# The intra-chunk scores of a recurrence, computed 64 keys at a time, with the two directions' masked scores added before the output matmuls

## The chip, the cores and the metric

The kernel runs on one core of one Trainium2 chip. The metric is the device time of one execution in microseconds (us), as the median over runs. A trace of one profiled execution of the kernel before the change is at hand.

## What is computed

The reference is one transformer block on 256 tokens of width 2048: a modulated norm, one wide projection, a recurrent branch (a gated linear recurrence that runs over the tokens forwards and backwards), a windowed attention branch, a gated merge and a convolutional feed-forward part. The change lies in the recurrent branch alone. It has eight heads of width 128. The sequence is cut into chunks of 64 tokens, and for each chunk, direction and head the reference computes (b is the running sum of log f inside the chunk)

```python
intra = jnp.einsum('bhncd,bhnsd->bhncs', q * jnp.exp(b - b_ref), k * jnp.exp(b_ref - b))
intra = jnp.where(tri, intra, 0.0)
o_intra = jnp.einsum('bhncs,bhnse->bhnce', intra, v)
...
o_n = jnp.einsum('bhcd,bhde->bhce', q_n, s)
s = d_n[..., None] * s + jnp.einsum('bhsd,bhse->bhde', k_n, v_n)
```

The backward direction is the same on flipped tokens, and the two outputs are added: `rms_norm(o_f + o_b, norm_g)`. So the masked scores of both directions are multiplied by the same values v and end in one sum.

## The kernel before the change

Weights stream from HBM in tiles of eight 128x128 blocks. SyncE (SP) issues the load of `raw` (L111), ScalarE (ACT) writes its rounded upper part `whi` (L112), VectorE (DVE) the rest `wlo` (L113), and TensorE (PE) multiplies with both (`mmul`, L68, in `duo`, `tform_all` and `natural`; results go to the PSUM tiles named `bankm`). This weight stream runs from start to end of the program. The rest is slipped in between: after every four steps of k a `tick()` takes one entry from a list of tasks. The Tile framework then orders the instructions of each engine by priority, so the order on an engine is fixed before the run.

For each head h the recurrent branch has these pieces:

- `hgrn_a(h, d, ps)`, once for each direction d, makes the decayed keys and queries from the projection: `KA` and `KB` are the keys of the two halves of each chunk, with zeros where the other half stands, `E1` the queries, `K_` the keys with the decay to the end of the chunk. `hgrn_q(h)` makes `QC`, the queries that meet the other chunk of a pair, and `K2`. All of it is DVE and ACT work on the tile `hb`.
- `hgrn_b(h)` (L555 to L577 before) computes the scores for two chunks at a time: key blocks of 128 tokens (a = 0, 1) for two directions, four squares of 128 keys by 128 queries in one PSUM bank `ips` (`banks<-hb` in the profile). For each square one matmul has all 128 keys of `KA` as weights and 128 queries moving, and a second has all 128 of `KB` and the 64 queries of one half of each chunk. Then four matmuls at L569 with 64 keys and 64 queries write the quarter of each square between its two chunks. One `copy_predicated` at L572 on DVE takes the four squares under a mask into `MI`, and six transposes at L576 (weights `hb`, `cst` is the identity in the names) turn the keys for the state update, which ACT copies out at L577.
- `hgrn_c(h)` (L579 to L588) updates the states: six matmuls at L584 and L585, then DVE at L586 and L588.
- `hgrn_d(h)` (L590 to L602) computes the output in one PSUM tile: four matmuls of `vn` with `MI` (`banks<-hb,vn`), one for each direction and key block, and four with the states `SS` (`banks<-hb`).
- `hgrn_e(h)` normalises the output one head later (L604 to L610).

All these matmuls are in fp32: each stands in the trace as two records (two passes), each with a weight load. A transpose has one record. The weight stream's matmuls (`bankm`) have one record each.

Two other users appear in the rows. `ada_mm` near the start multiplies 32 columns of weights (`csr`) with 256 or 512 moving columns; its sixteen steps of k are written to partitions 0, 32, 64 and 96 in turn. `ada()` (L378 to L398) is background work on DVE, with transposes at L391.

Of the kernel before, what the change touches and what calls it, by code (L numbers as in the profile page):

```python
# [9 lines left out]
U32 = mybir.dt.uint32  # L10
AF = mybir.ActivationFunctionType
ALU = mybir.AluOpType
AX = mybir.AxisListType

P = 128
# [6 lines left out]
CH = 64  # L22
# [28 lines left out]
def block_kernel(ctx, tc, xct, prm, cst, ada2, wst, out):  # L51
    nc = tc.nc
    V, S, PE = nc.vector, nc.scalar, nc.tensor
# [9 lines left out]
    def bank(pool=None):  # L63
        pool = pool or mm
        return pool.tile([P, 512], F32, name="bank" + ("m" if pool is mm else "s"))

    def mmul(o, l, r, start, stop):
        return PE.matmul(o, l, r, start=start, stop=stop, skip_group_check=True)  # L68
# [23 lines left out]
    def con(n):  # L92
        o, w = COFF[n]
        return cst_t[:, o:o + w]
# [85 lines left out]
    start = big.tile([P, 1024], F32, name="csr", tag="acc")  # L180
# [14 lines left out]
    def ada_mm(aps, u):  # L195
        n, per = len(chunks[u]), 4 // len(chunks[u])
        w = 256 * n
        for kt in range(KT):
            g, slot = 32 * (kt % 4), slots[groups[u][kt // 8 if n == 2 else 0] % 3][kt // per % 4]
            last_mm = mmul(aps[g:g + 32, 0:w], csr[:, kt, :], slot[:, kt % per * w:(kt % per + 1) * w], kt < 4, kt >= KT - 4)  # L200
        return last_mm
# [17 lines left out]
    def warm(n, after):  # L219
        with tc.issue_after(after.ins):  # L220
            for _ in range(n):
                last = mmul(ssq[:, 0:P], ident, ident, True, True)
        return last
# [35 lines left out]
    with tc.high_priority(offset=RUSH):  # L259
        for cnd in range(2):  # L260
            ts = slice(T * cnd, T * cnd + T)
# [4 lines left out]
    first = ada_mm(aps, 0)  # L266
    with tc.high_priority(offset=RUSH):
        first = warm(3, first)
# [9 lines left out]
    def unit(u):  # L278
        if len(chunks[u]) == 1:
            st.load(7)  # L280
            wv, w = [st.next(4)], [st.next() for _ in range(3)]
        else:
            st.load()
            wv = [st.next(4) for _ in range(2)]
            st.load(6)
            w = [st.next() for _ in range(6)]
        st.pos = 8
        return wv, w
# [19 lines left out]
    for u in range(len(chunks)):  # L308
        wv, w = unit(u)
# [42 lines left out]
    vn = big.tile([P, 4, 1024], F32, name="vn", tag="v")  # L352
# [121 lines left out]
    def carve():  # L474
        pos = [0]

        def take(n):
            r = hb[:, pos[0]:pos[0] + n]
            pos[0] += n
            return r  # L480
        return take

    take = carve()
    A_ = take(1024).rearrange("p (d t) -> p d t", d=2)
    K_ = take(1024).rearrange("p (d t) -> p d t", d=2)
    B_ = take(1024).rearrange("p (d t) -> p d t", d=2)
    E1 = take(512).rearrange("p (d t) -> p d t", d=2)
    KA = take(512).rearrange("p (d t) -> p d t", d=2)
    KB = take(512).rearrange("p (d t) -> p d t", d=2)
    QI = take(512).rearrange("p (d t) -> p d t", d=2)  # L490
    QC = take(256).rearrange("p (d a t) -> p d a t", d=2, a=2)
    K2 = take(256).rearrange("p (d t) -> p d t", d=2)
    KN = take(768).rearrange("p (d a e) -> p d a e", d=2, a=3)
    MI = take(512).rearrange("p (d a e) -> p d a e", d=2, a=2)
    SS = take(512).rearrange("p (n d e) -> p n d e", d=2, n=2)
    OS = take(512).rearrange("p (d t) -> p d t", d=2)
    for zt in (MI, KA, KB):
        V.memset(zt, 0.0)
# [54 lines left out]
            V.tensor_tensor(decb[:, d:d + 1], dec4[:, d, d, 0:1], dec4[:, d, d, 1:2], op=ALU.mult)  # L553

    def hgrn_b(h):  # L555
        ips = bank(ms)
        for d in range(2):
            for a in range(2):
                ts = slice(a * P, a * P + P)
                io = ips[:, (2 * d + a) * P:(2 * d + a + 1) * P]  # L560
                ih = io.rearrange("p (c h t) -> p c h t", c=2, h=2)[:, :, 1 - d, :]
                eh = E1[:, d, ts].rearrange("p (c h t) -> p c h t", c=2, h=2)[:, :, 1 - d, :]
                mmul(io, KA[:, d, ts], E1[:, d, ts], True, False)
                mmul(ih, KB[:, d, ts], eh, False, True)

        for d in range(2):
            c1, c2 = CH * d, CH * (1 - d)
            for a in range(2):
                PE.matmul(ips[c1:c1 + CH, (2 * d + a) * P + c2:(2 * d + a) * P + c2 + CH],  # L569
                          K_[:, d, a * P + c1:a * P + c1 + CH], QC[:, d, a], start=True, stop=True, skip_group_check=True)  # L570
        hm = con("hmask").bitcast(U32).rearrange("p (d e) -> p d e", d=2)[:, :, None, :].broadcast_to([P, 2, 2, P])
        V.copy_predicated(MI, hm, ips.rearrange("p (d a e) -> p d a e", d=2, a=2))  # L572
        for d in range(2):
            tp = bank(ms)
            for a, k in enumerate((K_[:, d, T:T + P], K_[:, d, T + P:], K2[:, d])):
                PE.transpose(tp[:, a * P:(a + 1) * P], k, ident)  # L576
            S.copy(KN[:, d], tp[:, 0:3 * P].rearrange("p (a e) -> p a e", a=3))  # L577

    def hgrn_c(h):  # L579
        hs = slice(h * P, h * P + P)  # L580
        sp = bank(ms).rearrange("p (n d e) -> p n d e", n=2, d=2)
        for d in range(2):
            for a in range(2):
                PE.matmul(sp[:, 0, d], KN[:, d, a], vn[:, 2 + a, hs], start=(a == 0), stop=(a == 1))  # L584
            PE.matmul(sp[:, 1, d], KN[:, d, 2], vn[:, d, hs], start=True, stop=True)  # L585
        V.tensor_copy(SS[:, 0], sp[:, 0])  # L586
        for d in range(2):
            V.scalar_tensor_tensor(SS[:, 1, d], SS[:, 0, d], decb[:, d:d + 1], sp[:, 1, d], op0=ALU.mult, op1=ALU.add)  # L588

    def hgrn_d(h):  # L590
        hs = slice(h * P, h * P + P)
        ob = bank(ms)
        obs[h] = ob
        first = True
        for d in range(2):
            for a in range(2):
                mmul(ob[:, a * P:a * P + P], vn[:, a, hs], MI[:, d, a, :], first, False)
                first = False
        for d in range(2):
            for a in range(2):  # L600
                mmul(ob[:, a * P:a * P + P], SS[:, a ^ d, d], QI[:, d, a * P:a * P + P], False, d == 1)
        S.activation(OS[:, 0], ob[:, 0:T], AF.Square)  # L602
# [58 lines left out]
    for h in range(H):  # L661
# [14 lines left out]
        for d in range(2):  # L676
            if 2 * h + d < 3:
                o = early_f[2 * h + d]
            else:
                o = bank()  # L680
                tform_all(o)
            hgrn_a(h, d, o)
            ada(1 if h > 5 or not h else 2)
        hgrn_q(h)
        parts = [lambda h=h: hgrn_e(h - 1), lambda h=h: hgrn_b(h), lambda h=h: hgrn_c(h), lambda h=h: hgrn_d(h)]
        if h == 0:

# [269 lines left out]
def _constants(np):  # L957
    c = np.zeros((P, CW), np.float32)

    def put(n, a):  # L960
        o, w = COFF[n]
        c[:, o:o + w] = a
    put("ident", np.eye(P, dtype=np.float32))
    put("ones", 1.0)
    pos = np.arange(T)
    inv = (np.float32(10000.0) ** (-np.arange(32, dtype=np.float32) / np.float32(32))).astype(np.float32)
    ar = ((pos // 64).astype(np.float32)[:, None] * inv).astype(np.float32)
    ac = ((pos % 64).astype(np.float32)[:, None] * inv).astype(np.float32)
    cc = np.concatenate([np.cos(ar), np.cos(ar), np.cos(ac), np.cos(ac)], 1)
    ss = np.concatenate([-np.sin(ar), np.sin(ar), -np.sin(ac), np.sin(ac)], 1)  # L970
    put("ropec", cc.reshape(2, P, P).transpose(1, 0, 2).reshape(P, 256))
    put("ropes", ss.reshape(2, P, P).transpose(1, 0, 2).reshape(P, 256))
    i, j = np.arange(P)[:, None], np.arange(P)[None, :]
    put("amask", np.concatenate([np.where(j <= i, 0.0, NEG), np.where(j >= i, 0.0, NEG)], 1))
    put("hmask", np.concatenate([i <= j, i >= j], 1).astype(np.float32))
    m = np.ones((1, T), np.float32)
    m[0, ::CH] = 0.0
    put("m64", m)
    return c
# [104 lines left out]
```

## Time and profile before

| | us |
|---|---|
| median of 3 runs | 1693.81 (1692.94 to 1693.84) |
| the profiled execution, its own time | 1692.48 |
| its span in the trace | 1690.7 |
| PE busy | 1677.4 (99% of the span) |
| PE weight loads (PEld) busy | 1425.9 (84%) |
| DVE busy | 1202.0 (71%) |
| ACT busy | 836.8 (49%) |

The span runs from the first to the last instruction; about 1.8 us of the execution lie outside it. PE and PEld are the two parts of TensorE, matmuls and weight loads. A record's duration is from its start to the end of its last result, so records of consecutive matmuls overlap: what a matmul costs a busy PE is the distance between starts, not its duration. The eight heads of the recurrence lie between about 134 and 479 us.

### The profile page before, as it was taken

Reading aid. Unit: us, or ns where it says so; the run is one execution under the profiler, and the core shown is the slowest. Engines: PE = TensorE matmul, PEld = TensorE weight load, DVE = VectorE, ACT = ScalarE, POOL = GpSimd, SP = SyncE. Lnnn points to the kernel's source line nnn. Section 1 sums busy time; section 2 is a strip of 40 time slices with the busy share of each in tenths; the row PEclk is TensorE's granted clock in tenths of the full one; section 3 lists DMA queues with packets and bytes.
Section 4 is the critical chain, followed back from the end, with each engine's and each line's share of the span. In section 5 each row is a group of like instructions: output and inputs, shape, how many; then the busy total and the mean of one; then the engine's idle time right before and its main releaser. Section 6 shows DMA issues by size and latency. Waiting matters only on the chain.

```text
span 1690.7 us, 24845 instructions
## 1 busy us (share of the span) xinstructions
PE 1677.4 (99%) x9486; PEld 1425.9 (84%) x9486; DVE 1202.0 (71%) x1896; ACT 836.8 (49%) x1279; POOL 68.8 (4%) x132
## 2 busy tenths in 40 slices
PE   8999999999999999999999999999999999999999
PEld 4668888888888888888888988888888888888887
DVE  3448975665879886878879887778666556666565
ACT  4337543443646664554554665555555435554332
POOL 0000100000000000000100000000000000000000
PEclk9999999999999999999999999999999999999999
DMA  9987733534466667877866577687555555555564
GB/s 379 408 343 257 270 125 129 193 102 152 158 195 204 212 223 245 293 257 267 280 216 232 180 240 261 211 277 250 192 187 188 187 188 188 194 190 187 187 200 149
DMA packets 104152, 371.84 MB, mean 220 GB/s; under 512 B 11488, under 2 KB 13920, under 8 KB 104032
## 3 DMA queue, kind: packets, MB, share of 16 engines
q1 hardware_dynamic: 85600, 303.14, 51.6%
q0 software_dynamic: 18432, 67.12, 12.7%
q8 instruction: 74, 1.21, 0.3%
q14 instruction: 46, 0.38, 0.1%
HBM read 368.11 MB, written 2.10 MB: 219 GB/s over the span
## 4 chain that ended last, share of the span: by engine, by line
PE 97%; DVE 1%; DMA 1%; issue 0%; ACT 0%; SPq 0%; DVEq 0%
PE bankm L68 89%; PE banks L68 6%; DMA ringv<-in_wst_dram 1%; PE banks L584 0%; PE banks L391 0%; PE banks L755 0%; DVE wlo L113 0%; PE banks L576 0%; DMA xraw<-in_xct_dram 0%; PE banks L585 0%; PE banks L209 0%; PE banks L569 0%; PE banks L608 0%; DVE acc L383 0%; PE banks L725 0%
## 5 line engine op out<-in xcount | busy, mean ns | idle before, releaser
L68 PE MATMUL bankm<-hl,whi 128*128 128x512 f32 (+1 forms) x3392 | 1050.6, 392 | 0.0
L113 DVE TENSOR_TENSOR wlo<-raw,whi 128x1024 fp32r<-128x1024 f32 (+1 forms) x498 | 606.5, 1219 | 324.4 <-ACT whi L112 323.0
L112 ACT CAST whi<-raw 128x1024 fp32r<-128x1024 f32 (+1 forms) x498 | 520.4, 1045 | 597.9 <-PE bankm L68 502.3
L68 PEld LDWEIGHTS bankm<-hl,wlo 128*128 128x128 f32 x3104 | 581.4, 188 | 131.9 <-DVE wlo L113 0.2
L68 PE MATMUL bankm<-hl,wlo 128*128 128x256 f32 (+2 forms) x3104 | 660.3, 287 | 0.0
L68 PEld LDWEIGHTS bankm<-hl,whi 128*128 128x128 f32 x3392 | 533.9, 189 | 19.9 <-DVE fs L873 0.3
L68 PE MATMUL bankm<-whi,hl 128*128 128x512 f32 x512 | 164.6, 395 | 1.0 <-ACT hl L230 0.9
L383 DVE SCALAR_TENSOR_TENSOR acc<-araw,csil,acc 128x1024 f32<-128x1024 f32 x120 | 153.3, 1278 | 1.8 <-DMA araw<-in_ada_dram 1.3
L68 PEld LDWEIGHTS bankm<-whi,hl 128*128 128x128 f32 x512 | 95.8, 188 | 22.4 <-ACT hl L230 2.6
L378 POOL DMA_DIRECT2D araw<-in_ada_dram x128 | 68.6, 536 | 1103.7 <-DVE acc L383 590.8
L68 PE MATMUL bankm<-wlo,hl 128*128 128x512 f32 x256 | 99.5, 391 | 0.0
L68 PE MATMUL bankm<-yb,whi 128*128 128x512 f32 x256 | 80.8, 397 | 0.0
L68 PE MATMUL bankm<-g,whi 128*128 128x512 f32 x256 | 80.4, 395 | 0.0
L68 PEld LDWEIGHTS bankm<-g,wlo 128*128 128x128 f32 x256 | 48.1, 188 | 11.4
L68 PEld LDWEIGHTS bankm<-yb,wlo 128*128 128x128 f32 x256 | 48.1, 188 | 11.3
L68 PEld LDWEIGHTS bankm<-wlo,hl 128*128 128x128 f32 x256 | 48.0, 188 | 9.8 <-DVE wlo L113 0.2
L904 DVE SCALAR_TENSOR_TENSOR xm<-bankm,modv,xm 128x256 f32<-128x256 f32 x96 | 42.1, 479 | 18.4 <-PE bankm L68 18.3
L886 ACT ACTIVATE fs<-fs,prm 128x256 f32<-128x256 f32 x44 | 26.5, 601 | 55.9 <-DVE fs L449 55.9
L68 PE MATMUL bankm<-yb,wlo 128*128 128x256 f32 x256 | 50.6, 279 | 0.0
L68 PE MATMUL bankm<-g,wlo 128*128 128x256 f32 x256 | 50.3, 278 | 0.0
L887 DVE SCALAR_TENSOR_TENSOR fs<-fs,prm,fs 128x255 f32<-128x255 f32 x44 | 21.3, 484 | 26.7 <-ACT fs L886 26.7
L211 DVE TENSOR_REDUCE tn<-banks 128x8 f32<-128x32 f32 (+1 forms) x9 | 1.7, 188 | 53.4 <-ACT whi L112 50.5
(218 smaller groups left out, 1227.7 us busy)
## 6 DMA issues: line engine op xcount, KB each, us to landing
raw<-in_wst_dram SPq DMA_DIRECT2D x489, 512.0 KB, 3.4
araw<-in_ada_dram POOLq DMA_DIRECT2D x128, 512.0 KB, 4.7
ringv<-in_wst_dram SPq DMA_DIRECT2D x24, 512.0 KB, 9.9
ringq<-in_wst_dram SPq DMA_DIRECT2D x20, 512.0 KB, 9.9
araw<-in_wst_dram SPq DMA_DIRECT2D x10, 512.0 KB, 9.9
xraw<-in_xct_dram SPq DMA_DIRECT2D x8, 512.0 KB, 6.8
raw<-in_wst_dram SPq DMA_DIRECT2D x7, 384.0 KB, 9.9
ringkT<-in_wst_dram SPq DMA_DIRECT2D x5, 512.0 KB, 9.9
```

The costliest lines, as they stand in the source:

```text
L68: return PE.matmul(o, l, r, start=start, stop=stop, skip_group_check=True)
L112: S.copy(hi, raw)
L113: self.last = V.tensor_tensor(lo, raw, hi.bitcast(F32), op=ALU.subtract)
L211: V.tensor_reduce(m8, aps[:, 0:w].rearrange("p (q g c) -> p q c g", q=2 * n, g=4)[:, :, 0:2, :], axis=AX.X, op=ALU.add)
L378: nc.gpsimd.dma_start(raw, ada2[idx])
L383: V.scalar_tensor_tensor(acc, raw, csil[:, kt, 0:1], acc, op0=ALU.mult, op1=ALU.add)
L886: S.activation(t, s, AF.Identity, bias=cb[:, f:f + 1], scale=cw[:, f, 1:2])
L887: V.scalar_tensor_tensor(t[:, 1:T], s[:, 0:T - 1], cw[:, f, 0:1], t[:, 1:T], op0=ALU.mult, op1=ALU.add)
L904: V.scalar_tensor_tensor(xm[:, j, :], o[:, T * i:T * i + T], gate2[:, j:j + 1], xm[:, j, :], op0=ALU.mult, op1=ALU.add)
```

## The change

`hgrn_b` lays the scores out in two PSUM areas x and y in place of four squares. x holds, for each key block a, one square of 128 keys by 128 queries: its two diagonal quarters have the forward scores inside the chunks, and the other two quarters the scores between the chunks, one quarter of each direction. y holds, for each a, 128 keys by 64 queries: the backward scores inside the chunks. Every matmul has 64 keys as weights and writes 64 partitions, 0 to 63 or 64 to 127, in turn: sixteen with `KA` (64 queries) and `KB` (32 queries), then four between the chunks. DVE masks x with one `copy_predicated` into `MI[:, 0]`, y with two of 64 partitions each into `MI[:, 1]`, and adds both into the new tile `MS`. `hgrn_d` multiplies `vn` with `MS`: two matmuls in place of four. The mask `hmask` in the constants has new values. Nothing else is edited.

```diff
+    MS = take(256).rearrange("p (a e) -> p a e", a=2)
...
     def hgrn_b(h):
         ips = bank(ms)
+        x, y = [ips[:, i * 2 * P:i * 2 * P + w].rearrange("p (a e) -> p a e", a=2) for i, w in ((0, 2 * P), (1, P))]
         for d in range(2):
             for a in range(2):
-                ts = slice(a * P, a * P + P)
-                io = ips[:, (2 * d + a) * P:(2 * d + a + 1) * P]
-                ih = io.rearrange("p (c h t) -> p c h t", c=2, h=2)[:, :, 1 - d, :]
-                eh = E1[:, d, ts].rearrange("p (c h t) -> p c h t", c=2, h=2)[:, :, 1 - d, :]
-                mmul(io, KA[:, d, ts], E1[:, d, ts], True, False)
-                mmul(ih, KB[:, d, ts], eh, False, True)
-
-        for d in range(2):
-            c1, c2 = CH * d, CH * (1 - d)
-            for a in range(2):
-                PE.matmul(ips[c1:c1 + CH, (2 * d + a) * P + c2:(2 * d + a) * P + c2 + CH],
-                          K_[:, d, a * P + c1:a * P + c1 + CH], QC[:, d, a], start=True, stop=True, skip_group_check=True)
-        hm = con("hmask").bitcast(U32).rearrange("p (d e) -> p d e", d=2)[:, :, None, :].broadcast_to([P, 2, 2, P])
-        V.copy_predicated(MI, hm, ips.rearrange("p (d a e) -> p d a e", d=2, a=2))
+                for kx, eh in ((KA, 0), (KB, CH // 2)):
+                    for c in range(2):
+                        ks, q0, w = slice(a * P + CH * c, a * P + CH * c + CH), (1 - d) * eh, CH - eh
+                        o = (y[CH * c:CH * c + CH, a, :] if d else x[CH * c:CH * c + CH, a, CH * c:CH * c + CH])[:, q0:q0 + w]
+                        mmul(o, kx[:, d, ks], E1[:, d, ks][:, q0:q0 + w], not eh, bool(eh))
+        for a in range(2):
+            for d in range(2):
+                c1, c2 = CH * d, CH * (1 - d)
+                mmul(x[c1:c1 + CH, a, c2:c2 + CH], K_[:, d, a * P + c1:a * P + c1 + CH], QC[:, d, a], True, True)
+        hm = con("hmask").bitcast(U32)
+        V.copy_predicated(MI[:, 0], hm[:, None, 0:P].broadcast_to([P, 2, P]), x)
+        for c in (0, CH):
+            V.copy_predicated(MI[c:c + CH, 1, :, c:c + CH], hm[c:c + CH, None, P:P + CH].broadcast_to([CH, 2, CH]), y[c:c + CH])
+        V.tensor_tensor(MS, MI[:, 0], MI[:, 1], op=ALU.add)
...
-        first = True
-        for d in range(2):
-            for a in range(2):
-                mmul(ob[:, a * P:a * P + P], vn[:, a, hs], MI[:, d, a, :], first, False)
-                first = False
+        for a in range(2):
+            mmul(ob[:, a * P:a * P + P], vn[:, a, hs], MS[:, a, :], a == 0, False)
```

The order that the framework writes for PE at the first head's scores and output. A row gives line, operation, tiles, and the output's shape (partitions x columns). Before:

```order
L68 MATMUL banks<-hb 128x128
L68 MATMUL banks<-hb 128x2x32
...
L569 MATMUL banks<-hb 64x64 x4
L576 MATMUL banks<-cst,hb 128x128 x6
...
L68 MATMUL banks<-hb,vn 128x128 x4
L68 MATMUL banks<-hb 128x128 x4
```

Now:

```order
L68 MATMUL banks<-hb 64x64 x2
L68 MATMUL banks<-hb 64x32 x2
...
L68 MATMUL banks<-hb 64x64 x4
L581 MATMUL banks<-cst,hb 128x128 x6
...
L68 MATMUL banks<-hb,vn 128x128 x2
L68 MATMUL banks<-hb 128x128 x4
```

The pairs of the first two rows are repeated four times in both. The block stands at the same place in the weight stream in heads 0 to 6. In heads 2 and 5 one transpose of the background work (L391) stands inside the block, behind its first matmul, before and now.

The last head on PE, before:

```order
L576 MATMUL banks<-cst,hb 128x128 x2
L68 MATMUL banks<-hb 128x128
L68 MATMUL banks<-hb 128x2x32
...
L569 MATMUL banks<-hb 64x64 x4
L576 MATMUL banks<-cst,hb 128x128
L68 MATMUL bankm<-whi,hl 128x512
```

Now:

```order
L581 MATMUL banks<-cst,hb 128x128 x2
L68 MATMUL bankm<-whi,hl 128x512
...
L68 MATMUL banks<-hb 64x64
L581 MATMUL banks<-cst,hb 128x128 x2
L68 MATMUL bankm<-wlo,hl 128x512
L581 MATMUL banks<-cst,hb 128x128
L68 MATMUL banks<-hb 64x64 x3
L68 MATMUL bankm<-whi,hl 128x512
```

Ten matmuls of the weight stream now stand between the first and the second direction's scores of this head, the matmuls between the chunks are split into one and three, `hgrn_c` into two pieces and `hgrn_d` into three.

The first head on DVE, with buffer numbers, before:

```order
L144 TENSOR_TENSOR qo_1038<-qo_1038,t_1254 128x512
L113 TENSOR_TENSOR wlo_1464<-raw_1462,whi_1463 128x1024
L572 COPY_PREDICATED hb_1259<-cst_77,banks_1372 128x512
L383 SCALAR_TENSOR_TENSOR acc_1140<-araw_1306,csil_82,acc_1140 128x1024
L516 TENSOR_SCALAR hb_1259<-hb_1259,lb1_t_1022,lb_t_1021 128x512
```

Now:

```order
L144 TENSOR_TENSOR qo_1038<-qo_1038,t_1254 128x512
L383 SCALAR_TENSOR_TENSOR acc_1140<-araw_1306,csil_82,acc_1140 128x1024
L574 COPY_PREDICATED hb_1259<-cst_77,banks_1372 128x256
L576 COPY_PREDICATED hb_1259<-cst_77,banks_1372 64x2x64
L113 TENSOR_TENSOR wlo_1475<-raw_1473,whi_1474 128x1024
L576 COPY_PREDICATED hb_1259<-cst_77,banks_1372 64x2x64
```

The lower weights `wlo_1464` (`wlo_1475` now) come behind one background operation and two of the new copies. On PE, in both orders, their first reader is the first `wlo` matmul behind the six matmuls of `hgrn_c(0)`. The orders of SP and POOL are the same as before.

## Rows read from the trace of the kernel before

**Rows 1.** The page: busy time of each engine, and the chain that ended last by engine.

```profile
PE 1677.4 (99%) x9486; PEld 1425.9 (84%) x9486; DVE 1202.0 (71%) x1896; ACT 836.8 (49%) x1279; POOL 68.8 (4%) x132
PE 97%; DVE 1%; DMA 1%; issue 0%; ACT 0%; SPq 0%; DVEq 0%
```

**Rows 2.** The waits in the stretch 130 to 480 us, longest first in total: who waited for whom, us in total, times, longest.

```profile
ACT whi L112 <- PE bankm L68: 117.5, 37, 5.7
...
PEld banks L68 <- DVE hb L534: 0.8, 1, 0.8
...
PE banks L68 <- DVE hb L534: 0.5, 1, 0.5
PEld banks L576 <- ACT hb L577: 0.3, 1, 0.3
...
PEld bankm L68 <- DVE wlo L113: 0.2, 1, 0.2
```

**Rows 3.** The timeline of PE around the scores of head 3: start us, duration us, engine, line, operation, out<-in, partitions*columns of the weights, moving shape, count of records merged into the row. Rows with different shapes but one line and tile are merged under the first one's shape.

```profile
266.57 0.39 PE L68 MATMUL bankm<-whi,hl 128*128 128x512 f32 x1
266.79 1.89 PE L68 MATMUL banks<-hb 128*128 128x128 f32 x16
268.62 0.46 PE L569 MATMUL banks<-hb 128*64 128x64 f32 x8
269.00 0.88 PE L576 MATMUL banks<-cst,hb 128*128 128x128 f32 x6
269.63 0.48 PE L68 MATMUL bankm<-whi,hl 128*128 128x512 f32 x1
```

**Rows 4.** The same eight records of L569 in four narrower windows of the timeline (those still running at 268.94, 269.00, 269.03 and 269.065 us), which shows the starts of the third, fifth, seventh and eighth.

```profile
268.72 0.35 PE L569 MATMUL banks<-hb 128*64 128x64 f32 x6
268.78 0.29 PE L569 MATMUL banks<-hb 128*64 128x64 f32 x4
268.84 0.23 PE L569 MATMUL banks<-hb 128*64 128x64 f32 x2
268.85 0.22 PE L569 MATMUL banks<-hb 128*64 128x64 f32 x1
```

**Rows 5.** Groups of PE's instructions by line and shape over the whole span: count | busy us, mean ns of one | idle before. The last row is of the weight loads.

```profile
L68 PE MATMUL banks<-ringv,csr 128*32 128x512 f32 x80 | 10.9, 596 | 0.5 <-DMA ringv<-in_wst_dram 0.5
L569 PE MATMUL banks<-hb 128*64 128x64 f32 x64 | 3.7, 234 | 0.0
L68 PEld LDWEIGHTS banks<-hb 128*128 128x128 f32 x192 | 23.5, 192 | 1.2 <-DVE hb L534 0.8
```

**Rows 6.** The timeline of PE at the output of head 3.

```profile
281.97 1.05 PE L68 MATMUL banks<-hb,vn 128*128 128x128 f32 x8
282.86 1.06 PE L68 MATMUL banks<-hb 128*128 128x128 f32 x8
283.67 0.48 PE L68 MATMUL bankm<-whi,hl 128*128 128x512 f32 x1
```

**Rows 7.** The timeline of PE where `ada_mm` follows the weight stream.

```profile
26.29 0.39 PE L68 MATMUL bankm<-whi,hl 128*128 128x512 f32 x1
26.61 0.41 PE L68 MATMUL banks<-ringq,csr 128*32 128x256 f32 x2
```

**Rows 8.** The timeline of PE around the scores of head 5, with a transpose of the background work inside.

```profile
367.43 0.47 PE L68 MATMUL bankm<-whi,hl 128*128 128x512 f32 x1
367.74 0.38 PE L68 MATMUL banks<-hb 128*128 128x128 f32 x2
367.96 0.27 PE L391 MATMUL banks<-cst,acc 128*128 128x128 f32 x1
368.07 1.67 PE L68 MATMUL banks<-hb 128*128 128x64 f32 x14
```

**Rows 9.** The timeline of PE around the scores of the last head; in brackets idle time and what ended it.

```profile
463.54 1.00 PE L68 MATMUL banks<-hb 128*128 128x128 f32 x8
464.38 0.39 PE L576 MATMUL banks<-cst,hb 128*128 128x128 f32 x2
465.30 1.10 PE L68 MATMUL banks<-hb 128*128 128x128 f32 x8 [0.53 <-DVE hb L534]
```

**Rows 10.** Groups of DVE's instructions by line and shape, columns as in rows 5.

```profile
L572 DVE COPY_PREDICATED hb<-cst,banks 128x512 f32<-128x512 uint32 x8 | 5.9, 732 | 0.1
L586 DVE COPY hb<-banks 128x256 f32<-128x256 f32 x8 | 3.3, 417 | 0.0
L588 DVE SCALAR_TENSOR_TENSOR hb<-hb,decb,banks 128x128 f32<-128x128 f32 x16 | 4.8, 343 | 0.2
L527 DVE TENSOR_TENSOR hb<-hb 128x256 f32<-128x256 f32 x16 | 6.7, 419 | 0.0
```

**Rows 11.** Busy time of the engines in three stretches of the recurrence: from:to, length, then us busy (and records) of PE, PEld, DVE, ACT and POOL, granted clock, DMA share, GB/s.

```profile
160.00:190.00 30.00, 30.00 (x194) 26.69 (x194) 30.00 (x46) 16.36 (x27) 4.24 (x8) 1.00 0.86 296
190.00:240.00 50.00, 50.00 (x264) 42.45 (x263) 38.37 (x84) 25.96 (x46) 2.65 (x5) 1.00 0.45 158
240.00:480.00 240.00, 239.47 (x1244) 202.66 (x1244) 159.73 (x303) 101.28 (x178) 16.32 (x30) 1.00 0.47 152
```

**Rows 12.** The timeline of DVE in the first head, and one row of PE's: the first reader of the weights written by DVE at 167.98.

```profile
167.98 1.22 DVE L113 TENSOR_TENSOR wlo<-raw,whi 128x1024 fp32r<-128x1024 f32 x1
169.12 0.73 DVE L572 COPY_PREDICATED hb<-cst,banks 128x512 f32<-128x512 uint32 x1
169.74 1.27 DVE L383 SCALAR_TENSOR_TENSOR acc<-araw,csil,acc 128x1024 f32<-128x1024 f32 x1
170.93 0.54 DVE L516 TENSOR_SCALAR hb<-hb,lb_t 128x512 f32<-128x512 f32 x1
...
174.55 0.40 PE L68 MATMUL bankm<-hl,wlo 128*128 128x256 f32 x2
```

More of the change, by code (lines that the diff above doesn't have):

```diff
@@ L974, in _constants @@
     put("amask", np.concatenate([np.where(j <= i, 0.0, NEG), np.where(j >= i, 0.0, NEG)], 1))
-    put("hmask", np.concatenate([i <= j, i >= j], 1).astype(np.float32))
+    put("hmask", np.concatenate([(i <= j) | (i // CH != j // CH), i % CH >= j], 1).astype(np.float32))
     m = np.ones((1, T), np.float32)
```

## The prediction

> **What bounds the kernel now.** I read the page first: PE is busy 99% of the span, and 97% of the chain that ended last is PE [rows 1]. Then the waits in the stretch of the recurrence, to see whether PE ever waits there: the long waits are ACT waiting for PE to free a weight buffer, while PE and its weight loads wait for others under 2 us in all [rows 2]. So this stretch lasts as long as PE's list of instructions, and a change is worth what it takes from that list, as long as DVE and ACT stay ahead. The price of an instruction on a busy PE is the distance to the next start, so I read distances from the timeline, not durations.
>
> **The scores, one head.** In head 3 the block takes 2.43 us, from the weight matmul at 266.57 to the first transpose at 269.00; the sixteen passes of `KA` and `KB` start between 266.79 and 268.62, 0.114 us each, and the eight passes of L569 take 0.38 [rows 3]. The `KB` passes, with half the moving columns, cost as much as the `KA` passes, so the 128-column weight load sets the pace, not the moving columns.
>
> The changed block is twenty matmuls of L569's kind, 64 columns of weights. The narrow windows show how these run: the third, fifth and seventh records start at 268.72, 268.78 and 268.84, and the eighth 0.01 behind the seventh [rows 4]. Two passes start nearly together, then 0.06 us pass. That is one pass for partitions 0 to 63 and one for 64 to 127, side by side: eight records of 0.234 us fit into 0.46 us. The 32-column matmuls of `ada_mm`, written to four groups of partitions in turn as the new code writes to two, show it too: 80 records of 596 ns, 47.7 us, lie in 10.9 us [rows 5]. So the twenty matmuls are ten in each half, twenty steps of two passes. The four of L569 took 0.38 us to the first transpose, with the slower first step (268.62 to 268.72) and the way out in it; sixteen more steps at 0.06 make 0.96. The way in, from a weight matmul to the first matmul with fewer columns, is 0.32 [rows 7]. New block: 0.32 + 0.38 + 0.96 = 1.66, against 2.43: **0.77 us less**. I take the 32-query passes at the same 0.06, since there the load should set the pace too; were it the moving columns, eight of the twenty steps would halve and save 0.24 more per head, 1.9 in all. That is the lower bound.
>
> **The output, one head.** Four matmuls of `vn` take 0.89 us, from 281.97 to 282.86 [rows 6]; two are left: **0.445 less**. Together 1.22 us per head.
>
> **The heads that differ.** In heads 2 and 5 a background transpose stands behind the first matmul [rows 8]. It cost little before, since all had full width; now PE leaves the narrow form and enters it again. The lone matmul spends two steps in one half alone (0.16 with the slow first step), the way out takes 0.15 (268.85 to 269.00) in place of 0.11 [rows 3, 4], and the second way in costs the 0.09 by which 0.32 [rows 7] is over the usual 0.23 behind a weight matmul (266.57 to 266.79 [rows 3]): 0.3 less gain, so 0.92 each.
>
> The last head is cut up: three narrow blocks instead of one, `hgrn_c` in two pieces, `hgrn_d` in three. Each further narrow block costs about 0.18 (0.09 on entry, 0.05 for the first step, 0.04 on leaving), and uneven pieces add two steps: about 0.5. Against it, PE idles 0.53 us there for the second direction's queries (L534) [rows 9], and ten weight matmuls now stand in that place. I take 1.0 for this head, between 0.4 (the wait comes back elsewhere) and 1.4.
>
> **DVE.** One copy of 0.73 goes. The new one of 256 columns I price by the copy at L586, 0.42, the two of 64 partitions by L588, the nearest with 128 columns out of PSUM, 0.34 at most each, and the addition by L527, 0.42 [rows 10]: 1.52, so 0.79 more per head, 6.3 in all. I cost this at nothing. What covers it: between 240 and 480 us DVE is busy 160 of 240; only at 160 to 190, in the first head, is it full, 30.00 of 30 [rows 11]. There the weights made at 167.98 are first read at 174.55 [rows 12]. In the new order they come behind one background operation (1.2) and two copies (0.7), so at about 171.1; PE gets there 0.8 earlier, at 173.8. Cover is left, 2.7 us. `MS` is ready long before its reader: the mask copy of that head ended at 169.8 and the output comes some 10 us later. ACT, the DMA queues and the background work on POOL keep their orders or their place near PE's. Without that cover, each 0.1 us by which DVE is late is 0.1 us of PE.
>
> **Sum.** Heads 0, 1, 3, 4 and 6: 5 x 1.22 = 6.1. Heads 2 and 5: 1.8. Head 7: 1.0. Together 8.9 us from the profiled execution's 1692.48, which lies 1.33 under the median of 1693.81; from the median, **1684.9 us**. Behind the recurrence nothing changes, and PE stays the bound, so I carry the gain to the end.
>
> **Rivals.**
>
> *The halves do not run side by side in the new order (slower).* L569 is in order half by half, two matmuls each; the new code alternates with every matmul and adds onto the same partitions. If each pass had to wait for the one before, with its load not hidden, it would cost the first step's 0.10 [rows 3, 4]: 0.32 + 40 x 0.10 + 0.15 = 4.47, 2.04 more than now, less 0.445 in the output: 1.6 more per head, 12.8 in all, 1706.6. The point from which it decides is 0.06 us per single pass: there 40 passes eat the whole gain. Against it: `ada_mm` alternates in the same way, adds onto the same partitions, and four of its passes run at once [rows 5]. Chance 0.04. [...]
>
> *Side by side only in part (no change).* One pass after another, but with hidden loads, 0.06 each: 0.32 + 2.4 + 0.1 = 2.8, 0.4 more than now, which the output's 0.445 pays back: about 1693.5. Chance 0.06.
>
> *DVE becomes the bound in places.* If the first two heads and the last wait for DVE after all, their gain of 3.4 is lost (1688.3), and if the 0.79 shows on PE in all three, 2.4 more (1690.7). For it: DVE is full at 160 to 190, and its order there puts weights behind new copies. Against it: the 2.7 us of cover. Chance 0.12.
>
> **How the numbers follow.** My forecast has the remaining 0.78. Its own range is 1682 (32-query passes at half price, the last head at its best, a run at the low end of the runs shown) to 1687 (the last head at 0.4, switches somewhat dearer). The range of 1681.5 to 1689.5 takes in most of the DVE case and leaves out the two cases in which the halves don't share PE. A measurement of this kernel tells some 0.2%, 3.4 us, from no change. Faster by more than that: the forecast and most of the DVE case, 0.88. Within it: the half-way case and the rest of the DVE case, 0.08. Slower: 0.04.
>
> **What would show it.** Right: `banks<-hb` records with 64 columns in pairs 0.01 us apart, pairs 0.06 apart; about 1.66 us from weight matmul to transposes in head 3 and 0.45 for the four `vn` passes; still no waits of PE for `wlo`. Wrong: pairs 0.1 or more apart, idle time of PE before weight matmuls in the first head with DVE named, or a longer wait before the output for `MS`.

## The result, and the profile after

The changed kernel takes **1683.56 us** (median of six runs, 1683.46 to 1684.77), against 1693.13 (1692.10 to 1693.84) for the kernel before in the same series: ratio 0.9948, 95% interval 0.9937 to 0.9958, so 9.6 us faster. The forecast was 1684.9, its range 1681.5 to 1689.5. Both profiled executions agree with this: 1692.48 before, 1683.52 now, spans 1690.7 and 1681.7.

The page answers to [rows 1]. PE is still the bound, with a shorter list in time though it has 96 records more; DVE is busy 4.5 us more.

```profile
PE 1668.9 (99%) x9582; PEld 1415.0 (84%) x9582; DVE 1206.5 (72%) x1920; ACT 835.1 (50%) x1279; POOL 68.6 (4%) x132
PE 97%; DVE 1%; DMA 1%; ACT 0%; issue 0%; SPq 0%; DVEq 0%
```

**Scores of head 3.** The timeline of PE, answering to [rows 3], then a narrow window of the forty records (at 263.68 us; a row starts with the earliest record still running and counts those that are), and two of their weight loads (at 264.295 and 264.353):

```profile
263.08 0.39 PE L68 MATMUL bankm<-whi,hl 128*128 128x512 f32 x1
263.40 1.39 PE L68 MATMUL banks<-hb 128*64 128x64 f32 x40
264.72 0.88 PE L581 MATMUL banks<-cst,hb 128*128 128x128 f32 x6
...
263.51 0.40 PE L68 MATMUL banks<-hb 128*64 128x64 f32 x8
...
264.16 0.26 PEld L68 LDWEIGHTS banks<-hb 128*64 128x64 f32 x5
...
264.22 0.26 PEld L68 LDWEIGHTS banks<-hb 128*64 128x64 f32 x5
```

From the weight matmul to the first transpose now pass 264.72 - 263.08 = 1.64 us; it was 2.43. Forecast was 1.66. A record lasts 0.20 to 0.27, and eight run at once: they start in twos, 7 ns apart by their raw starts (263.402 and 263.409), and a step of two takes (1.32 - 0.15) / 20 = 0.058, with the way out, 0.15, taken off. That is a mean: the starts of successive pairs lie 0.03 to 0.11 apart (raw starts), while the weight loads of a half start 0.06 apart (264.16, 264.22). The way in is 0.32, as taken.

**By shape**, answering to [rows 5]: the narrow matmuls and, in the last row, their loads, 138 ns each against 192 for 128 columns.

```profile
L68 PE MATMUL banks<-hb 128*64 128x64 f32 x192 | 12.1, 236 | 0.2 <-DVE hb L535 0.2
L68 PE MATMUL banks<-hb 128*64 128x32 f32 x128 | 8.0, 210 | 0.0
L68 PEld LDWEIGHTS banks<-hb 128*64 128x64 f32 x320 | 10.6, 138 | 3.5 <-issue 2.3 <-DVE hb L535 0.6 <-DVE hb L549 0.3
```

**Output of head 3**, answering to [rows 6]: the first output matmul with `MS` to the first with the states, 278.14 - 277.70 = 0.44 for four passes; it was 0.89 for eight.

```profile
277.70 0.60 PE L68 MATMUL banks<-hb,vn 128*128 128x128 f32 x4
278.14 1.06 PE L68 MATMUL banks<-hb 128*128 128x128 f32 x8
```

**Scores of head 5**, answering to [rows 8]. One matmul (two records), then the background transpose, then the other nineteen. The way in takes 361.90 - 361.49 = 0.41, and 0.52 pass from the lone matmul's start to the rest.

```profile
361.49 0.48 PE L68 MATMUL bankm<-whi,hl 128*128 128x512 f32 x1
361.90 0.33 PE L68 MATMUL banks<-hb 128*64 128x64 f32 x2
362.16 0.33 PE L391 MATMUL banks<-cst,acc 128*128 128x128 f32 x1
362.42 1.38 PE L68 MATMUL banks<-hb 128*64 128x64 f32 x38
363.72 0.87 PE L581 MATMUL banks<-cst,hb 128*128 128x128 f32 x6
```

**Last head**, answering to [rows 9]: three narrow blocks, and 0.15 of the 0.53 us of waiting for the queries is left.

```profile
455.61 0.66 PE L68 MATMUL banks<-hb 128*64 128x64 f32 x16
...
459.09 0.80 PE L68 MATMUL banks<-hb 128*64 128x64 f32 x18 [0.15 <-DVE hb L535]
...
460.54 0.45 PE L68 MATMUL banks<-hb 128*64 128x64 f32 x6
```

**DVE.** Its new groups by shape, answering to [rows 10]:

```profile
L574 DVE COPY_PREDICATED hb<-cst,banks 128x256 f32<-128x256 uint32 x8 | 3.6, 447 | 0.0
L576 DVE COPY_PREDICATED hb<-cst,banks 64x128 f32<-64x128 uint32 x16 | 4.7, 296 | 0.1
L577 DVE TENSOR_TENSOR hb<-hb 128x256 f32<-128x256 f32 x8 | 3.4, 421 | 0.1
```

The stretch in which it is full, answering to [rows 11] (us busy of PE, PEld, DVE, ACT and POOL):

```profile
160.00:190.00 30.00, 30.00 (x211) 26.39 (x210) 29.91 (x49) 15.93 (x26) 3.71 (x7) 1.00 0.85 289
```

The weights behind the first mask copies in the first head, and the first matmul that reads them, answering to [rows 12]:

```profile
169.59 1.21 DVE L113 TENSOR_TENSOR wlo<-raw,whi 128x1024 fp32r<-128x1024 f32 x1
...
173.59 0.40 PE L68 MATMUL bankm<-hl,wlo 128*128 128x256 f32 x2
```

The four new operations take 0.447 + 2 x 0.296 + 0.421 = 1.46 per head (forecast 1.52) for one copy of 0.73. The weights end at 170.80 and are read at 173.59: 2.8 us of cover, where 2.7 was forecast.

**Where the 9 us went.** The weight stream has 8324 matmuls in both traces, so the same one can be looked up in each. The 413th, shortly before the first head's scores, starts 0.15 us earlier now (160.06 and 159.91; nothing of PE's list is changed ahead of it); the last one before the last head's block at 463.31 before and 455.29 now, 8.02 earlier; the 1691st, behind the recurrence, at 500.04 and 491.08, 8.96; from there on the difference stays at 8.95. So the change made 8.96 - 0.15 = **8.8 us**, all of it in the eight heads. Below, "in the recurrence" means this difference between these two matmuls, which leaves those 0.15 out.

### The profile page after: what moved, and what is told of

Read it like the earlier page. It is cut to its first block, busy times and chain, and to the rows that moved or that the text cites. A ratio compares the mean times of both kernels' runs of the same rounds, so it can differ in the third digit from the quotient of the medians.

```text
span 1681.7 us, 25059 instructions
## 1 busy us (share of the span) xinstructions
PE 1668.9 (99%) x9582; PEld 1415.0 (84%) x9582; DVE 1206.5 (72%) x1920; ACT 835.1 (50%) x1279; POOL 68.6 (4%) x132
## 4 chain that ended last, share of the span: by engine, by line
PE 97%; DVE 1%; DMA 1%; ACT 0%; issue 0%; SPq 0%; DVEq 0%
PE bankm L68 90%; PE banks L68 5%; DMA ringv<-in_wst_dram 1%; PE banks L391 0%; PE banks L589 0%; PE banks L758 0%; DVE wlo L113 0%; PE banks L581 0%; DMA xraw<-in_xct_dram 0%; PE banks L590 0%; PE banks L209 0%; PE banks L611 0%; PE banks L728 0%; DVE acc L383 0%; ACT t L245 0%
```

## The experiments

The theory: PE's list is the time; score matmuls with 64 keys run in pairs, one in each half of the partitions; a step lasts as long as a weight load needs; DVE is covered. The rivals: the halves do not share PE in every order, the moving columns set the pace, DVE has become the bound.

**1. Scores alone.** The change without `MS`:

```diff
-        V.tensor_tensor(MS, MI[:, 0], MI[:, 1], op=ALU.add)
...
-        for a in range(2):
-            mmul(ob[:, a * P:a * P + P], vn[:, a, hs], MS[:, a, :], a == 0, False)
+        first = True
+        for d in range(2):
+            for a in range(2):
+                mmul(ob[:, a * P:a * P + P], vn[:, a, hs], MI[:, d, a, :], first, False)
+                first = False
```

> The scores part of the change alone: twenty matmuls with 64 keys each and the three mask copies as in the changed kernel, but no MS; the output reads both directions' masks with four vn matmuls, as before. Theory (PE's list is the time, and each part of the change is worth what it takes off that list): the output's 0.446 us per head come back, 8 x 0.446 = 3.57, so 1683.56 + 3.57 = 1687.1 us, and vn passes 0.89 us in all per head. Rival (the output was hidden beside DVE or ACT work, and the whole gain is the scores' block): within 0.5 of the changed kernel, 1683.6.

Measured: 1687.03 (ratio to before 0.9966, interval 0.9954 to 0.9979), and in the recurrence 5.4 us less than before.

**2. Output alone.** The kernel before, with the sum:

```diff
+        V.tensor_tensor(MS, MI[:, 0], MI[:, 1], op=ALU.add)
...
+        for a in range(2):
+            mmul(ob[:, a * P:a * P + P], vn[:, a, hs], MS[:, a, :], a == 0, False)
```

> The output part alone: scores and the one mask copy as in the kernel before, and then the addition of the two directions into MS on VectorE and two vn matmuls in place of four. Theory: 3.57 us off the time before, 1693.13 - 3.57 = 1689.6, and together with the scores alone it makes up the whole change (6.0 + 3.6 = 9.6). Rival (the two matmuls only gave room to a wait that the scores' part needs too, so the parts are not additive): no change here, 1693.1.

Measured: 1689.32 (0.9980, 0.9970 to 0.9989), against 1692.51 for the kernel before in that series; in the recurrence 3.4 less. The two parts add up: 5.4 + 3.4 is the whole change's 8.8. Both rivals fall: neither part was hidden.

**3. Half by half.**

```diff
-        for d in range(2):
-            for a in range(2):
-                for kx, eh in ((KA, 0), (KB, CH // 2)):
-                    for c in range(2):
+        for c in range(2):
+            for d in range(2):
+                for a in range(2):
+                    for kx, eh in ((KA, 0), (KB, CH // 2)):
...
-        for a in range(2):
-            for d in range(2):
+        for d in range(2):
+            for a in range(2):
                 c1, c2 = CH * d, CH * (1 - d)
```

> The changed kernel with the same twenty score matmuls in another order: all ten that write partitions 0 to 63 first, then the ten of 64 to 127. It tells what the side-by-side run of the two halves rests on. Theory A (each half has its own place in line and PE reaches far ahead in its list for the other half): as the changed kernel, 1683.6, block of head 3 1.63 us. Theory B (neighbours in program order share the array, and PE looks only a few passes ahead, as L569's eight passes before showed: two matmuls per half, in order half by half, ran side by side): ten matmuls one after the other in a half, mostly alone, 36 or more of 40 passes at 0.058 instead of 20 steps: block 1.63 + 16 to 20 x 0.058 = 2.6 to 2.8, so 0.93 to 1.16 per head, 7.4 to 9.3 us slower than the changed kernel, 1691 to 1693.

That text has the order wrong: this kernel writes eight matmuls for one half, eight for the other, then two and two, not ten and ten. Measured: 1689.92 (0.9980, 0.9971 to 0.9989), 5.2 us slower than the changed kernel in the recurrence. The timeline of head 3, and then narrow windows at 267.60, 267.95 and 268.30:

```profile
267.01 2.10 PE L68 MATMUL banks<-hb 128*64 128x64 f32 x40
269.05 0.88 PE L581 MATMUL banks<-cst,hb 128*128 128x128 f32 x6
...
267.41 0.40 PE L68 MATMUL banks<-hb 128*64 128x32 f32 x4
...
267.73 0.42 PE L68 MATMUL banks<-hb 128*64 128x64 f32 x8
...
268.13 0.34 PE L68 MATMUL banks<-hb 128*64 128x32 f32 x3
```

Three or four records run where eight did, except in the middle. The first record of the second half starts with the thirteenth of the first half's sixteen passes: PE took it up when four passes stood ahead of it. With that reach the list gives 12 lone steps, 4 pairs, 8 lone, 4 pairs, 4 lone = 32 in place of 20, so 12 x 0.058 = 0.70 more; measured are 2.04 in place of 1.32. Theory B holds, with 12 steps for its 16 to 20.

**4 and 5. By twos, by fours.** A reach of four passes foretells two other orders (the cross matmuls go by twos in both):

```diff
             for a in range(2):
-                for kx, eh in ((KA, 0), (KB, CH // 2)):
-                    for c in range(2):
+                for c in range(2):
+                    for kx, eh in ((KA, 0), (KB, CH // 2)):
```

```diff
         for d in range(2):
-            for a in range(2):
-                for kx, eh in ((KA, 0), (KB, CH // 2)):
-                    for c in range(2):
+            for c in range(2):
+                for a in range(2):
+                    for kx, eh in ((KA, 0), (KB, CH // 2)):
```

> The changed kernel with its score matmuls written two for partitions 0 to 63, two for 64 to 127, and so on (KA and KB of one quarter together), the cross ones likewise. After the half-by-half run the model is: PE takes up a pass for the free half when it stands at most four passes (two matmuls) behind the one that runs. Model: pairs all the way, twenty steps, block of head 3 as in the changed kernel, 1.32 us from the first narrow matmul to the first transpose; 1683.6. Rival (only the very next matmul is taken up): every second matmul runs alone at the start of its pair, some 28 to 30 steps, 0.5 more per head, 1687 to 1688.

> The same in fours: four score matmuls (eight passes) for partitions 0 to 63, four for 64 to 127, again four and four, then two and two. Model (four passes ahead): 4 passes alone, then pairs, 4 alone at the end: 24 steps in place of 20, so 4 x 0.058 = 0.23 more per head: 1.32 + 0.23 = 1.55 us from the first narrow matmul to the first transpose in head 3, and 1.9 in all, 1685.4. Rival (PE looks further ahead than two matmuls): 1.32 and 1683.6. Rival (one matmul): 30 steps or more, 1.9 us, 1688.

Measured: 1684.01 by twos, 1685.78 (0.9959, 0.9945 to 0.9974) by fours. In the recurrence that is 0.2 and 2.1 us slower than the changed kernel. The blocks of head 3, first by twos, then by fours:

```profile
263.93 1.41 PE L68 MATMUL banks<-hb 128*64 128x64 f32 x40
265.27 0.87 PE L581 MATMUL banks<-cst,hb 128*128 128x128 f32 x6
```

```profile
264.07 1.69 PE L68 MATMUL banks<-hb 128*64 128x64 f32 x40
265.69 0.88 PE L581 MATMUL banks<-cst,hb 128*128 128x128 f32 x6
```

1.34 and 1.62 us: by twos nothing is lost, by fours 0.30 where the reach gave 0.23. The rivals (a reach of one matmul, or an unlimited one) fall. All these matmuls have two passes, so the runs do not tell whether PE counts passes or matmuls.

**6. All 64 queries in `KB`.**

```diff
-                        ks, q0, w = slice(a * P + CH * c, a * P + CH * c + CH), (1 - d) * eh, CH - eh
+                        ks, q0, w = slice(a * P + CH * c, a * P + CH * c + CH), 0, CH
...
-                        mmul(o, kx[:, d, ks], E1[:, d, ks][:, q0:q0 + w], not eh, bool(eh))
+                        mmul(o, kx[:, d, ks], (QI if eh else E1)[:, d, ks][:, q0:q0 + w], not eh, bool(eh))
```

> The changed kernel with all 64 queries as moving data in its KB matmuls too, in place of 32 (the moving data are taken from QI there, so the scores of this kernel are other numbers). It tells what sets the 0.058 us of a step: the weight load (64 columns in every step) or the moving columns. Theory A (the load): a KB step costs what a KA step costs already, so nothing changes: block of head 3 1.63 us, 1683.6. Theory B (the columns: 32-query steps at about half): the block's eight KB steps get 0.03 longer each, 0.24 per head, 1.9 us slower, 1685.5.

Measured: 1684.10 (1683.59 to 1685.65). Forty records of 64 columns take what the mixed ones took, 266.67 - 265.35 = 1.32:

```profile
265.35 1.39 PE L68 MATMUL banks<-hb 128*64 128x64 f32 x40
266.67 0.88 PE L581 MATMUL banks<-cst,hb 128*128 128x128 f32 x6
```

So between 32 and 64 the moving columns do not set the pace of a load of 64 columns. The 0.5 us in the median is not in the blocks; the last section shows where it arises in the profiled execution.

**7. 32 keys as weights.** If a half has a pace of its own, a quarter should too:

```diff
-                for kx, eh in ((KA, 0), (KB, CH // 2)):
-                    for c in range(2):
...
+                for g in range(4):
+                    c, r = g // 2, 32 * g
+                    o = y[r:r + 32, a, :] if d else x[r:r + 32, a, CH * c:CH * c + CH]
+                    qs = E1[:, d, a * P + CH * c:a * P + CH * c + CH]
+                    if g % 2 == d:
+                        mmul(o, KA[:, d, a * P + r:a * P + r + 32], qs, True, True)
+                    else:
+                        mmul(o.rearrange("p (h t) -> p h t", h=2), KB[:, d, a * P + r:a * P + r + 32],
+                             qs[:, None, (1 - d) * 32:(1 - d) * 32 + 32].broadcast_to([P, 2, 32]), True, True)
...
+                for r in (CH * d, CH * d + 32):
+                    mmul(x[r:r + 32, a, CH * (1 - d):CH * (1 - d) + CH], K_[:, d, a * P + r:a * P + r + 32], QC[:, d, a], True, True)
```

> The changed kernel with its cut taken one step further: 32 keys as weights in place of 64, so that four groups of partitions are written in turn (24 score matmuls per head in place of 20, six for each group; nothing else changes). In the changed kernel a step (one pass in each half) costs 0.058 us, and in the half-by-half order a pass alone in its half also cost 0.058, so the limit is a half's own. Theory A (each column group has its own pace, 0.058 per pass): 12 steps in place of 20, 0.46 less per head, 3.7 in all: 1683.6 - 3.7 = 1679.9 us. Theory B (PE starts a pass no more often than every 0.029 us, as it does now with both halves busy): 48 passes in place of 40, 0.23 more per head, 1.9 in all: 1685.4. Theory C (the pace follows the width of the weights, 0.03 for 32 columns, with all four groups side by side): 0.8 less per head, 1677.2.

Measured: **1679.74** (ratio to before 0.9924, 0.9911 to 0.9936). Theory A said 1679.9. Head 3, and a narrow window at 262.50 with sixteen records running at once:

```profile
262.14 0.88 PE L68 MATMUL banks<-hb 128*32 128x64 f32 x48
262.95 0.87 PE L585 MATMUL banks<-cst,hb 128*128 128x128 f32 x6
...
262.29 0.44 PE L68 MATMUL banks<-hb 128*32 128x64 f32 x16
```

0.81 us for 48 passes, 0.51 less than the changed kernel's 1.32 (8 steps x 0.058 = 0.46). B is out, since four passes start 7 ns apart (raw starts) where B allows one per 0.029 us. C's time is out too: a step is not halved. That does not yet tell what the load of 32 columns alone would allow, because every pass here has 64 moving columns (those with `KB` take 32 queries twice); the last section comes back to it.

**8. More work for DVE.**

```diff
-        V.tensor_tensor(MS, MI[:, 0], MI[:, 1], op=ALU.add)
+        for _ in range(4):
+            V.tensor_tensor(MS, MI[:, 0], MI[:, 1], op=ALU.add)
```

> The changed kernel with the addition into MS done four times, which adds three times 0.42 us of VectorE per head, 1.26, more than the 0.73 that the change itself added. Theory (VectorE is covered: weights in the first head are ready 2.8 us before PE reads them, and MS many us before the output): 1683.6, within 0.5. Rival (VectorE's added work costs time in the heads in which it is full, the first two and the last): up to 3 x 1.26 = 3.8 us, 1687.4.

Measured: 1684.08 (1683.64 to 1684.84). 10 us more of DVE cost 0.3 in the recurrence. The loss lies in head 1: its scores take 210.53 - 208.99 = 1.54 us in place of 1.32, since the weight loads stop in the middle (timelines of PE and of the loads; in brackets idle time and what ended it):

```profile
208.99 1.62 PE L68 MATMUL banks<-hb 128*64 128x64 f32 x40
210.53 1.03 PE L582 MATMUL banks<-cst,hb 128*128 128x128 f32 x6
...
209.69 0.43 PEld L68 LDWEIGHTS banks<-hb 128*64 128x64 f32 x12 [0.15 <-DVE hb L535]
```

So DVE is covered with the change's load, and the thinnest cover is not the one that the prediction names (first head, 2.8 us): it is that of the second direction's queries (L535) in head 1, where 1.26 us more are too much by some 0.2. The transposes behind them wait another 0.2 for DVE at L614, and the last head, in a slightly other order, gives 0.1 back.

**9. Blocks of heads 2 and 5 kept whole.**

```diff
+        with (tc.high_priority(offset=24) if h in (2, 5) else nullcontext()):
...
```

> The changed kernel with the score matmuls of heads 2 and 5 put ahead by a priority, so that the background transpose L391 no longer stands behind the first of the twenty; the block then lies whole between weight matmuls, apart from the transposes L581. Theory (L391 there costs 0.4 us per head over the steady heads, since PE leaves the narrow form and enters it once more): 0.4 x 2 = 0.8 less, 1682.8. Rival (each change of form costs the same wherever it is, and one is spent anew at the block's own end, between block and transposes): 0.4 less at most, 1683.2 to 1683.6.

Measured: 1683.01 (1682.65 to 1684.73), in the recurrence 0.6 less than the changed kernel, 0.3 per head. That lies between the theory's 0.8 and the rival's 0.4 at most, so neither is right as it stands: leaving the form once less is worth this much here.

**10. Both (7 and 9).**

> Both at once: 32 keys as weights, and the blocks of heads 2 and 5 kept whole. If both work as their theories say: 1683.6 - 3.7 - 0.8 = 1679.1 us. If 32 keys are paced by the start of passes: 1685.4 - 0.8 = 1684.6, or a little under that since the pieces of heads 2 and 5 are shorter.

Measured: 1679.91 (1678.56 to 1680.40; ratio 0.9923, 0.9910 to 0.9937). In the recurrence it is 0.6 under experiment 7, as experiment 9 was under the changed kernel; the medians (1679.91 and 1679.74) can't tell the two. Both beat the kernel before and the changed one; experiment 7 is the simpler.

**11. Narrow matmuls one by one.** The edit of 9 for all heads:

```diff
+        with tc.high_priority(offset=24):
...
```

> The changed kernel with its twenty score matmuls put ahead in every head; the order that results sets them singly between weight matmuls in heads 0, 1, 3, 4, 6 and 7 (105 narrow pieces in place of 12), and whole in heads 2 and 5. It prices the way into the narrow form and out of it, the terms with which the prediction costed heads 2, 5 and 7. Theory (each change of form is paid, also under long weight matmuls): a lone narrow matmul takes 0.318 (way in) + 0.106 (its second pass) + 0.153 (way out) = 0.58 from weight matmul to weight matmul where 0.23 is usual, 0.35 each; some 98 of them 34 us, less the 8.6 that the same matmuls cost in their blocks: 25 us slower than the changed kernel, about 1709. Rival (a long weight matmul beside it hides the change of form, and a lone matmul costs its two passes, 0.11): about 2 us slower, 1686.

Measured: 1722.27 (1.0178, 1.0161 to 1.0195). In the recurrence 36.7 us slower than the changed kernel, more than the theory's 25. The timeline of head 1:

```profile
211.86 0.33 PE L68 MATMUL banks<-hb 128*64 128x64 f32 x2
212.12 0.51 PE L68 MATMUL bankm<-hl,whi 128*128 128x512 f32 x1
212.55 0.30 PE L68 MATMUL banks<-hb 128*64 128x32 f32 x2
...
215.92 0.30 PE L68 MATMUL banks<-hb 128*64 128x32 f32 x2
216.15 0.50 PE L68 MATMUL bankm<-hl,whi 128*128 128x512 f32 x1
216.48 0.39 PE L68 MATMUL bankm<-hl,wlo 128*128 128x512 f32 x1
216.71 0.40 PE L68 MATMUL bankm<-hl,whi 128*128 128x512 f32 x1
217.04 0.34 PE L68 MATMUL banks<-hb 128*64 128x64 f32 x4
```

With one weight matmul between two narrow ones a round takes 0.66 to 0.69 us (212.55 - 211.86 = 0.69), 0.43 to 0.46 more than the 0.23 of a weight matmul alone. With three between it takes 217.04 - 215.92 = 1.12, also 0.43 more than three of them. The theory lacks a term: the first weight matmul behind a narrow one has 0.33 to the next (216.15 to 216.48) in place of 0.23, and where a narrow one follows it at once, the way in shows 0.43 (212.12 to 212.55) in place of 0.32. This 0.10 per piece, for some 98 pieces, is 10 of the 12 us by which the theory fell short. The rival, that long matmuls hide the change of form, falls.

## Why the prediction was right

Its steps, in us taken off:

| step | forecast | measured |
|---|---|---|
| heads 0, 1, 3, 4, 6, each | 1.22 | 1.25 |
| heads 2 and 5, each | 0.92 | 0.84 |
| head 7 | 1.0 | 0.94 |
| DVE's added work | 0 | 0 |
| sum | 8.9 | 8.8 |

The steady heads are read between the weight matmuls before and after (3.07 to 2.27 us for the scores, 1.93 to 1.48 for the output, from the raw starts); heads 2 and 5 likewise (3.26 to 2.87, and the output); head 7 is 8.96 - 8.02. The measured rows add up to 8.87; the other 0.06 goes in small shifts between the heads.

- **The scores.** The pair of passes per 0.06, read from L569's eight records [rows 4] and from `ada_mm` [rows 5], carried over to twenty matmuls that alternate and add onto the same partitions. Experiments 3 to 5 show the condition that I had not named: the next matmul for the free half must stand within four passes. Alternating by ones, as the change does, is far inside; L569 by twos was inside just so, which is why its rows could be used.
- **32-query passes at the price of 64.** Right, by experiment 6. The lower bound of 1.9 us was not needed. That the `KB` passes before cost as much as the `KA` passes does not follow from the mean of 0.114 in [rows 3]; what bears it out is that their weight loads start 0.11 apart throughout (raw starts of that trace).
- **The output.** 0.446 per head for 0.445, and by itself 3.4 for 3.6 (experiment 2).
- **Heads 2 and 5: the step mis-sized.** The way into the block costs 0.09 to 0.10 more, as in a steady head: it is 0.41 now and was 0.31 before (367.43 to 367.74 [rows 8]), both behind a weight matmul that follows a transpose. What I priced too low is the transpose inside. From the lone matmul to the other nineteen pass 0.52, and those take 1.30 (362.42 to 363.72) where a whole block takes 1.32: 0.50 more, against 0.11 for the transpose before (367.96 to 368.07 [rows 8]). So it costs 0.39, where I had 0.16 + 0.04 + 0.09 = 0.29. Two terms were short. The way out of 0.15 comes in place of the 0.06 that I had charged for that step, not of 0.11, so it adds 0.09 and not 0.04. And from the transpose to the next narrow pass it is 0.26 (362.16 to 362.42), 0.15 more than before, not 0.09.
- **Head 7.** 0.94 for 1.0. That 1.0 was a choice between 0.4 and 1.4, so the near hit bears out none of its terms.
- **DVE at nothing.** Right, by the cover forecast for the first head and by experiment 8, though the thinnest cover was elsewhere.
- **The rivals.** The halves do share PE: of the slower one's 0.10 per single pass, 0.029 was measured (1.16 / 40). Half by half, though, a reordering of the very same matmuls gives back 5.2 of the 8.8 us: what the middle rival feared is real, but a matter of order. What decided was how near in PE's list a matmul for the free half stood: four passes ahead was within reach (experiments 3 to 5). The matmuls did not all start in the order of the list: in experiment 3 the second half's first matmul stands behind the sixteenth pass of the first half and starts 5 ns after the thirteenth (raw starts; the records do not name their half, but up to there they start singly and the next ones in pairs).
- **The total.** Measured 1683.56 lies 1.3 under the forecast: 0.7 is the starting point (the kernel before at 1693.13 in that series, not 1693.81), the rest is of the size by which executions differ (1683.46 to 1684.77).

## What to carry to other kernels

When weights of 128 columns are only partly useful, and the loads set the pace, cut them so that column groups of 64 or 32 are written in turn: a step keeps its price (0.058 us here for 64 columns of weights and 0.055 for 32, with up to 64 moving columns) and does two or four passes. Write the groups alternately, by ones or twos (1.32 and 1.34 us a block here; 1.62 by fours, 2.04 half by half), and keep the narrow matmuls together, since each stray one between wide matmuls costs 0.43 to 0.46 us (experiment 11). For an engine that is not the bound, look for the thinnest cover along every chain, not only where it is busiest.

## What was not expected

- **A step costs nearly the same for 64 and for 32 columns of weights**: 0.058 and (0.81 - 0.15) / 12 = 0.055 us. A pass alone in its half costs a whole step too: by the model of experiment 3 its block has 32 steps, (2.04 - 0.15) / 32 = 0.059 each. With 32 columns of weights the step goes with the moving columns, though: in the trace of before, `ada_mm` starts its groups of four 0.22 us apart with 256 moving columns (two narrow windows, at 27.05 and 27.258), some four times the 0.055 of experiment 7 with 64. So in experiment 7 the moving columns rather than the load may set the pace; at 64 columns of weights the two limits would then lie close together. A kernel with 32 keys and only 32 queries in its `KB` passes would tell; it was not run.

```profile
26.85 0.40 PE L68 MATMUL banks<-ringq,csr 128*32 128x256 f32 x4
...
27.07 0.40 PE L68 MATMUL banks<-ringq,csr 128*32 128x256 f32 x4
```

- **The way in adds some 0.1 us in all three places that the traces show**: 0.32 in place of 0.23 behind a run of wide matmuls, 0.41 in place of 0.31 behind one that follows a transpose (head 5 and [rows 8]), 0.43 in place of 0.33 behind one that itself follows narrow ones (experiment 11). The last two are long without any change of form ahead: the weight matmul behind a transpose or a narrow piece has more than 0.23 to the next one in any case (the 0.31 and the 0.33).

**Where an execution's extra 1 to 2 us come from.** In some profiled executions DVE waits longer for the background load `araw` (L381) in the first head; the full DVE then hands its delay to PE through `wlo`. In experiment 6, whose profiled run was its slowest (1685.65), the waits at 140 to 170 us are these (us in total, times, longest):

```profile
DVE acc L381 <- DMA araw<-in_ada_dram: 3.2, 1, 3.2
PEld bankm L68 <- DVE wlo L113: 2.5, 2, 1.3
PE bankm L68 <- DVE wlo L113: 1.6, 2, 0.8
```

and in the changed kernel's own trace these:

```profile
DVE acc L381 <- DMA araw<-in_ada_dram: 1.2, 1, 1.2
PEld bankm L68 <- DVE wlo L113: 0.3, 1, 0.3
```

The profiled runs of experiments 3 and 11 have it as well (2.7 and 2.8 for `araw`). Why the load is late there is open.
